# Low halves of four weight matrices kept in DRAM between two token streams, and the second prelude cut in two

## The chip, the cores and the metric

The kernel runs on one core of one Trainium2 chip. The metric is the device time of one execution in microseconds (us). A core has a matrix engine PE with a weight-load path (PEld), a vector engine DVE, a scalar engine ACT, a general engine POOL, and SP, which here issues every DMA, in program order, on one hardware queue (q1 in the profile). A DMA that waits for something on SP holds back those behind it.

## The reference

Two requests ("streams", 512 tokens by 1024 channels each, stream 0 and stream 1) go through the same two layers with the same weights. Layer 0 is a bidirectional RWKV-7 time mixing:

```python
xx = 0.5 * (x_prev + x_next) - xn
lerp = lambda j: xn + xx * mu[j]
r = heads(lerp(0) @ w_r)
k = heads(lerp(1) @ w_k)
v = heads(lerp(2) @ w_v)
z = xn @ w_z
for d in range(2):
    xw = lerp(3 + d)
    xa = lerp(5 + d)
    w_log = -softplus(-(w0[d] + tanh(xw @ w1[d]) @ w2[d])) - 0.5
    a = sigmoid(a0[d] + (xa @ a1[d]) @ a2[d])
    ys.append(_wkv7_scan(r, decay, k_d, v, -kk, kk * a, reverse=(d == 1)))
out = (norm(ys[0] + ys[1]) + bonus) * silu(z)
return out @ w_o
```

Layer 1 is a gated neighbourhood attention (w_in, four products a column block, then w_o). Each layer has an RMS norm before and after it.

## The kernel before

Activations stand with channels on the 128 partitions and 512 tokens along the row. A weight matrix of 1024x1024 is eight "columns" of 128 output channels; a column is loaded as two halves of 128x512 f32 (256 KB, tile `raw`).

A product is done in three passes of reduced precision: each operand x is split into hi = x rounded (tile `whi` for a weight, a cast on ACT) and lo = x - hi (tile `wlo`, a subtraction on DVE), and PE adds hi*hi, hi*lo and lo*hi. So a column takes 8 x 3 = 24 matmuls of 128x512, and each half column costs one cast and one subtraction. `wlo` and `whi` have four buffers each (NW = 4), `raw` three. The same weights are split once for stream 0 and again for stream 1.

The program has three parts.

**The prelude** (generator `prelude`, method `columns`). For stream s it loads x, makes the norm (sum of squares, `rstds`), the shift xx, the low-rank product (L549 to L551, 96 matmuls: tanh(xw @ w1) and xa @ a1 for both directions) with its output chain (L560 to L572: tiles `lm` and `lr`, one buffer each; the `hid` rows of stream 1 are stored from `lr`), and the shifted inputs (L581, tile `ls` of four buffers, also used for the splits of the low-rank input of stream 1), which are stored and read again later. Beside it run the eight z and the eight k columns of stream 0 (L423 to L425). A scheduler of the compiler orders this part.

**The scan phase** (`scan_phase`). Its order is recorded by hand for PE, DVE and ACT: `weave` asks a list of threads in turn, with a model clock, which can go on. Threads are the steps of the scan (8 blocks of 8 steps; L1068, L1090, L1162, L1189, L1209, L1213), `preps` (the inputs of a block: L872, L873, then DVE and ACT work up to the tile `ab`), `inverse` (a triangular inverse in many small DVE operations, L994, L996), `finish`, and `flow`, which keeps PE busy in between with the remaining products (L802 to L804): r and v of stream 0, then k, r, v and z of stream 1, then w_o and six column blocks of layer 1's w_in. In `flow` the thread `loads` fetches `raw`, `splits` casts (L721) and subtracts (L723), and `products` multiplies. If the clock foresees a gap, a dummy matmul (L1622) is put in, so that PE does not go idle. SP's DMAs are not in the hand-made order; they follow the scheduler.

**The rest** (`rest`) is the second layer and the end.

A block's preparation needs the column sums of all k columns (`rn`) and the r columns of the block; the first scan step needs the first block's preparation, its inverse and its v columns.

Of the kernel before, what the change touches and what calls it, by code (L numbers as in the profile page):

```python
# [19 lines left out]
P = 128  # L20
# [209 lines left out]
class Trunk:  # L230
# [172 lines left out]
    def split(self, raws, j):  # L403
        hi, lo = (self.t(tag, (P, self.WP), self.NW, F32R) for tag in ("whi", "wlo"))
        self.halves(raws[j], lo, hi, self.nc.vector if j % 2 else self.nc.vector)
# [85 lines left out]
    def prelude(self, s):  # L491
# [5 lines left out]
        for k in range(KT):  # L497
            if s == 0 and k == self.WFIRST:
                self.first = [self.weight(self.a["w_z"][0])]
# [36 lines left out]
        self.shift[s] = xn, xx  # L536

        pm = self.p("pf", (P, 2, T))
# [39 lines left out]
        for kind, j in (("v", 2),) if s == 0 else (("k", 1), ("r", 0), ("v", 2)):  # L578
            for k in range(KT):
                t = self.t("ls", (P, T), 4, F32, self.lp)  # L580
                vt.scalar_tensor_tensor(t, xx[k], self.vec("mu", 8 * j + k), xn[k], op0=ALU.mult, op1=ALU.add)  # L581
                self.save("l" + kind, s, k, t)
                yield
# [106 lines left out]
    def columns(self, s, kind, x, ps=range(NP)):  # L690
        for p in ps:
            w = self.first.pop() if self.first else self.weight(self.a["w_" + kind][p])
            ps = yield from self.gemm(w, x, self.gt)
            for _ in self.column(s, kind, p, ps):
                pass
            yield

    def flow(self):
# [3 lines left out]
        cols = [(g, j, src, done) for g, (_, _, c) in enumerate(self.groups) for j, (src, done) in enumerate(c)]  # L702
# [14 lines left out]
        def splits():  # L717
            for h in range(2 * len(cols)):
                yield "A", lambda: h < did["load"] and h < did["k"] // 4 + self.NW, lambda c: c.at(name(raw[h]))
                hi, lo = (self.t(tag, (P, self.WP), self.NW, F32R) for tag in ("whi", "wlo"))  # L720
                nc.scalar.copy(hi, raw[h])  # L721
                yield "D"
                nc.vector.tensor_tensor(lo, raw.pop(h), hi.bitcast(F32), op=ALU.subtract)  # L723
# [844 lines left out]
    def stream(self):  # L1568
# [3 lines left out]
            (self.a["w_" + kind][p], lambda ps, p=p: self.column(s, kind, p, ps)) for p in ps]  # L1572
# [3 lines left out]
        def x1n(k):  # L1576
# [11 lines left out]
            (now, self.xr, cols(0, "r")), (now, disk("lv", 0), cols(0, "v")), (now, disk("lk", 1), cols(1, "k")),  # L1588
# [123 lines left out]
    def run(self):  # L1712
# [85 lines left out]
def both(*gs):  # L1798
    for g in gs:
        yield from g  # L1800
# [110 lines left out]
```

## Time and profile before

| what | us |
|---|---|
| median of three runs (lowest, highest) | 1689.23 (1682.6, 1691.78) |
| the profiled execution, its own time | 1683.88 |
| its span, first to last instruction | 1682.1 |
| first matmul of the prelude | 8.8 |
| first and last start of a dummy matmul (L1622) | 171.4, 987.1 |
| first and last start of a product of the scan phase (L802) | 173.9, 1179.6 |
| DVE subtractions of weights, scan phase (L723, x160) | 108.7 |
| DVE subtractions of weights, elsewhere (L373, x148) | 101.4 |

A row of a group view reads: line, engine, operation, output<-input, shapes, count | busy us, mean ns of one | idle time of the engine just before, and what ended most of it. A row of the stage table has the stage in us, its length, and for each engine the busy time and the number of instructions, then the granted PE clock (1.00 is full), the busy share of the 16 DMA engines and the GB/s moved. A row of a timeline has the start, the length, the instruction and, in brackets, the idle time ahead of it with what ended it. A row of waits has total us, times and the longest. PE's records overlap, since a matmul starts before the one ahead of it has left the array, so the distance of two starts is what one costs.

### The profile page before, as it was taken

Reading aid. Unit: us, or ns where it says so; the run is one execution under the profiler, and the core shown is the slowest. Engines: PE = TensorE matmul, PEld = TensorE weight load, DVE = VectorE, ACT = ScalarE, POOL = GpSimd, SP = SyncE. Lnnn points to the kernel's source line nnn. Section 1 sums busy time; section 2 is a strip of 40 time slices with the busy share of each in tenths; the row PEclk is TensorE's granted clock in tenths of the full one; section 3 lists DMA queues with packets and bytes.
Section 4 is the critical chain, followed back from the end, with each engine's and each line's share of the span. In section 5 each row is a group of like instructions: output and inputs, shape, how many; then the busy total and the mean of one; then the engine's idle time right before and its main releaser. Section 6 shows DMA issues by size and latency. Waiting matters only on the chain.

```text
span 1682.1 us, 46291 instructions
## 1 busy us (share of the span) xinstructions
PE 1570.9 (93%) x18818; PEld 1201.2 (71%) x18818; DVE 1227.8 (73%) x2725; ACT 984.0 (58%) x1977; POOL 24.1 (1%) x94
## 2 busy tenths in 40 slices
PE   7989898899989998989998999999999899999998
PEld 6767666676766776767765767777777687777776
DVE  8985668688777697887888887865576856555564
ACT  5443655676655667755674665454577655555562
POOL 0000000000000000000000000000000000000000
PEclk9989999899999999999997999999999999999999
DMA  5435678678586786876776665554774347555553
GB/s 209 163 125 187 203 243 261 202 228 257 170 262 211 225 255 205 259 243 205 241 232 214 202 199 199 184 178 131 267 231 155 111 127 249 182 157 175 164 181 107
DMA packets 240821, 336.26 MB, mean 200 GB/s; under 512 B 53696, under 2 KB 119360, under 8 KB 240608
## 3 DMA queue, kind: packets, MB, share of 16 engines
q1 hardware_dynamic: 240608, 333.31, 61.6%
q8 instruction: 148, 2.42, 0.6%
q14 instruction: 65, 0.53, 0.1%
HBM read 227.71 MB, written 105.51 MB: 198 GB/s over the span
## 4 chain that ended last, share of the span: by engine, by line
PE 67%; DVE 11%; DMA 9%; ACT 8%; issue 4%; SPq 1%; DVEq 0%; POOL 0%; ACTq 0%; POOLq 0%
PE pm L802 7%; PE pg L423 6%; PE pg L424 6%; PE pg L425 6%; PE pm L804 5%; PE pm L803 5%; PE pf L1090 2%; PE sc L1433 2%; PE us L1209 2%; DMA cab<-dab 2%; PE po L1466 2%; PE pt L1451 2%; PE zy L1162 2%; PE us L1189 2%; PE zy L1213 1%
## 5 line engine op out<-in xcount | busy, mean ns | idle before, releaser
L802 PE MATMUL pm<-act,whi 128*128 128x512 f32 x640 | 287.6, 449 | 16.1 <-ACT act L771 7.2
L804 PE MATMUL pm<-act,wlo 128*128 128x512 f32 x640 | 256.7, 401 | 12.2 <-DVE wlo L723 12.2
L803 PE MATMUL pm<-act,whi 128*128 128x512 f32 x640 | 258.0, 403 | 5.1 <-DVE act L749 4.2
L423 PE MATMUL pg<-act,whi 128*128 128x512 f32 x448 | 182.4, 408 | 5.9 <-ACT act L372 5.5
L424 PE MATMUL pg<-act,whi 128*128 128x512 f32 x448 | 178.1, 398 | 0.1
L425 PE MATMUL pg<-act,wlo 128*128 128x512 f32 x448 | 177.5, 396 | 0.0
L802 PEld LDWEIGHTS pm<-act,whi 128*128 128x128 f32 x640 | 122.6, 192 | 63.8 <-issue 16.1
L372 ACT CAST whi<-raw 128x512 fp32r<-128x512 f32 x148 | 91.4, 619 | 129.3 <-PE pg L424 75.3
L804 PEld LDWEIGHTS pm<-act,wlo 128*128 128x128 f32 x640 | 123.4, 193 | 44.3 <-DVE wlo L723 16.9
L373 DVE TENSOR_TENSOR wlo<-raw,whi 128x512 fp32r<-128x512 f32 x148 | 101.4, 687 | 70.2 <-ACT whi L372 63.0
L803 PEld LDWEIGHTS pm<-act,whi 128*128 128x128 f32 x640 | 123.6, 193 | 29.6 <-DVE act L749 7.2
L723 DVE TENSOR_TENSOR wlo<-raw,whi 128x512 fp32r<-128x512 f32 x160 | 108.7, 684 | 42.9 <-ACT whi L721 39.5
L721 ACT CAST whi<-raw 128x512 fp32r<-128x512 f32 x160 | 98.1, 616 | 51.7 <-PE pm L803 14.5
L423 PEld LDWEIGHTS pg<-act,whi 128*128 128x128 f32 x448 | 84.8, 190 | 24.8 <-ACT act L372 6.1
L425 PEld LDWEIGHTS pg<-act,wlo 128*128 128x128 f32 x448 | 84.8, 189 | 17.9 <-issue 0.8
L424 PEld LDWEIGHTS pg<-act,whi 128*128 128x128 f32 x448 | 84.9, 190 | 17.4 <-issue 2.0
L996 DVE TENSOR_TENSOR N<-etmp,N 128x30 f32<-128x30 f32 (+14 forms) x240 | 78.5, 327 | 4.2
L994 DVE TENSOR_TENSOR etmp<-N 128x30 f32<-128x30 f32 (+14 forms) x240 | 78.3, 326 | 4.2
L1444 DVE CUSTOM_DVE_ANT_0 sb<-sc,bias 128x256 f32<-128x256 f32 x128 | 49.2, 419 | 31.1 <-PE pt L1451 23.5
L1090 PE MATMUL pf<-cab 64*64 64x128 f32 (+1 forms) x2048 | 67.9, 268 | 2.2 <-issue 2.1
L1447 ACT ACTIVATE sb<-sb,mx 128x256 f32<-128x256 f32 x128 | 63.9, 504 | 9.1 <-DVE mx L1446 9.0
L1113 DVE TENSOR_TENSOR AK<-zy,cc 128x256 f32<-128x256 f32 x63 | 26.6, 421 | 53.5 <-PE zy L1068 51.6
(389 smaller groups left out, 3389.7 us busy)
## 6 DMA issues: line engine op xcount, KB each, us to landing
dab<-ab SPq DMA_DIRECT2D x32, 1024.0 KB, 5.5
cab<-dab SPq DMA_DIRECT2D x64, 512.0 KB, 4.4
raw<-in_w_in_dram SPq DMA_DIRECT2D x128, 256.0 KB, 3.3
bias<-in_rpb_dram SPq DMA_DIRECT2D x32, 384.0 KB, 4.8
raw<-in_w_z_dram SPq DMA_DIRECT2D x32, 256.0 KB, 4.5
dz<-tmp SPq DMA_DIRECT2D x32, 256.0 KB, 3.0
raw<-in_w_k_dram SPq DMA_DIRECT2D x32, 256.0 KB, 4.0
dk<-tmp SPq DMA_DIRECT2D x32, 256.0 KB, 2.2
```

What stands on the lines that cost most here:

```text
L372: self.nc.scalar.copy(hi, src)
L373: (eng or self.nc.vector).tensor_tensor(lo, src, hi.bitcast(F32), op=ALU.subtract)
L423: nc.tensor.matmul(ps, hi, x[k][0], start=(k == 0), stop=False)
L424: nc.tensor.matmul(ps, hi, x[k][1], start=False, stop=False)
L425: nc.tensor.matmul(ps, lo, x[k][0], start=False, stop=(k == KT - 1))
L721: nc.scalar.copy(hi, raw[h])
L723: nc.vector.tensor_tensor(lo, raw.pop(h), hi.bitcast(F32), op=ALU.subtract)
L802: nc.tensor.matmul(ps, hi[:, at], xh, start=(k == 0), stop=False)
L803: nc.tensor.matmul(ps, hi[:, at], xl, start=False, stop=False)
L804: nc.tensor.matmul(ps, lo[:, at], xh, start=False, stop=(k == KT - 1))
L996: vt.tensor_tensor(N[:, q + 1:, :q], tv, N[:, q + 1:, :q], op=ALU.add)
L1090: end = nc.tensor.matmul(st.f[half(a), h, 0, d, g] if st.last else st.f[half(a), h, :, d, g], ab[half(h), d, g, 2 * e[d] + 1 - a], rt if s ...
```

## The change

Two things are changed.

**Low halves through DRAM.** Where stream 0 splits a half column of w_z, w_k, w_r or w_v, the low half is also stored to a DRAM tile (`lower_half`, 64 stores of 256 KB). Where stream 1 needs the same half column, `splits` loads it into `wlo` from there instead of subtracting; the cast on ACT stays, and `raw` is still loaded for it.

**The prelude.** Stream 0's prelude runs to its end first, at 0.6 of a step for each step of the z columns. Then the k columns run beside the first part of stream 1's prelude (norm, shift, the k, r and v shifts) and the v shifts of stream 0. Then the first four r columns of stream 0 run in the prelude too, written beside the low-rank product of stream 1, and the scan phase's first group has the other four.

```diff
+    PACE, EARLY = (0.95, 0.8), 4
...
+        self.wlow = {}
...
-    def weight(self, src):
+    def weight(self, src, key=None):
...
             for j in range(len(raws)):
                 out += self.split(raws, j)
+                if key:
+                    self.lower_half(key, j, self.low)
         return out
+
+    def lower_half(self, key, j, lo):
+
+        self.wlow[key, j] = d = self.dram("wl%s%d%d" % (*key, j), (P, self.WP))
+        self.nc.sync.dma_start(d, lo.bitcast(F32))
...
         self.shift[s] = xn, xx
-
+        if s == 1:
+            yield from self.shifts(1, (("k", 1), ("r", 0), ("v", 2)))
+        else:
+            yield from self.low_rank(0)
+
+    def low_rank(self, s):
...
         def splits():
             for h in range(2 * len(cols)):
-                yield "A", lambda: h < did["load"] and h < did["k"] // 4 + self.NW, lambda c: c.at(name(raw[h]))
+                key, j = keys[h // 2], h % 2
+                room = lambda: h < did["k"] // 4 + self.NW
+                yield "A" if (key, j) not in self.wlow else "S", lambda: room() and h < did["load"], (
+                    (lambda c: c.at(name(raw[h]))) if (key, j) not in self.wlow else None)
                 hi, lo = (self.t(tag, (P, self.WP), self.NW, F32R) for tag in ("whi", "wlo"))
-                nc.scalar.copy(hi, raw[h])
-                yield "D"
-                nc.vector.tensor_tensor(lo, raw.pop(h), hi.bitcast(F32), op=ALU.subtract)
+                if (key, j) in self.wlow:
+                    self.load(lo.bitcast(F32), self.wlow[key, j])
+                    yield "A", None, lambda c: c.at(name(raw[h]))
+                    nc.scalar.copy(hi, raw.pop(h))
+                else:
+                    nc.scalar.copy(hi, raw[h])
+                    yield "D"
+                    nc.vector.tensor_tensor(lo, raw.pop(h), hi.bitcast(F32), op=ALU.subtract)
+                    if key:
+                        self.lower_half(key, j, lo)
...
-            (now, self.xr, cols(0, "r")), (now, disk("lv", 0), cols(0, "v")), (now, disk("lk", 1), cols(1, "k")),
+            (now, self.xr, cols(0, "r", range(self.EARLY, NP))), (now, disk("lv", 0), cols(0, "v")), (now, disk("lk", 1), cols(1, "k")),
...
-        a = both(a, self.prelude(1))
-        run(self.columns(0, "z", self.xz), (a, 1))
-        run(self.columns(0, "k", self.shifted(0, 1)), (a, 1))
+        run(self.columns(0, "z", self.xz), (a, 0.6))
+        run(a)
+        x = self.shifted(0, 1)
+        a = both(self.prelude(1), self.shifts(0, (("v", 2),)))
+        run(self.columns(0, "k", x), (a, self.PACE[0]))
         run(a)
         self.xr = self.shifted(0, 0)
+        a = self.low_rank(1)
+        run(self.columns(0, "r", self.xr, range(self.EARLY)), (a, self.PACE[1]))
+        run(a)
         first.close()
```

The order of the built programs shows where this puts the work. In these rows a tile's number tells its buffers apart.

PE, at the end of the prelude, in the kernel before: L646 is the last operation of a k column, L1622 the dummy, L802 to L804 the first r column (pm_1734), L872 and L873 the first matmuls of the first preparation.

```order
L646 MATMUL pm_1626<-tmp_1624,cc 2x512
L1622 MATMUL zy_1710<-cc 128x256 x6
L802 MATMUL pm_1734<-act_1641,whi_1725 128x512
L803 MATMUL pm_1734<-act_1640,whi_1725 128x512
L804 MATMUL pm_1734<-act_1641,wlo_1726 128x512
...
L804 MATMUL pm_1774<-act_1683,wlo_1803 128x512
L1622 MATMUL zy_1710<-cc 128x256 x2
L872 MATMUL pm_1835<-h_126_633,w2h_1793 128x512
L873 MATMUL pm_1835<-h_126_633,w2l_1792 128x512
```

The same place in the changed kernel: L433 to L435 end the fourth r column, L568 to L570 are the low-rank product of stream 1 (pf_1614, pm_1615, us_1616), L835 to L837 the fifth r column, L905 and L906 the first preparation.

```order
L435 MATMUL zy_1893<-act_1588,wlo_1888 128x512
L1655 MATMUL zy_1954<-cc 128x256 x6
L568 MATMUL pf_1614<-ls_1617,lw_359 128x512
L568 MATMUL pm_1615<-ls_1617,lw_345 128x512
L568 MATMUL us_1616<-ls_1617,lw_395 128x512
L835 MATMUL pm_1995<-act_1546,whi_1984 128x512
...
L570 MATMUL pf_1614<-ls_1822,lw_421 128x512
L569 MATMUL us_1616<-ls_1823,lw_399 128x512
L570 MATMUL us_1616<-ls_1822,lw_400 128x512
L905 MATMUL pm_2014<-h_172_797,w2h_1972 128x512
L906 MATMUL pm_2014<-h_172_797,w2l_1971 128x512
```

The low-rank product of stream 1, which lay among the k columns, now lies in one piece behind the fourth r column, with the first 12 matmuls of the fifth among it, and the first preparation follows at once.

DVE, at the same time, in the kernel before: L563, L565 and L570 are the output chain of the low-rank product, L581 the shifts, L599 and L373 the r operands, L854 and L858 open the first preparation.

```order
L570 TENSOR_TENSOR lr_1277<-pm_1050,lm_1276 128x512
L581 SCALAR_TENSOR_TENSOR ls_1434<-xx_988,cv,xn_759 128x512
...
L563 TENSOR_TENSOR lr_1297<-lm_1296 128x512
L373 TENSOR_TENSOR act_1652<-xr_1650,act_1653 128x512
L599 SCALAR_TENSOR_TENSOR xr_1662<-xx_402,cv,xn_119 128x512
...
L570 TENSOR_TENSOR lr_1297<-us_1051,lm_1296 128x512
...
L854 SCALAR_TENSOR_TENSOR rb_1788<-k_1786,cv,rb_1788 128x512
L858 TENSOR_TENSOR w2l_1792<-tmp_1794,w2h_1793 128x512
```

In the changed kernel (L603 the shifts, L375 the splits of the low-rank input, L582, L584 and L589 the output chain, L887 and L891 the preparation):

```order
L603 SCALAR_TENSOR_TENSOR ls_1512<-xx_525,cv,xn_141 128x512
L375 TENSOR_TENSOR ls_1618<-xn_892,ls_1617 128x512
...
L375 TENSOR_TENSOR ls_1823<-xn_906,ls_1822 128x512
L582 TENSOR_TENSOR lr_1848<-lm_1847 128x512
L584 SCALAR_TENSOR_TENSOR lm_1847<-lr_1848,lm_1847 128x512
L589 TENSOR_TENSOR lr_1848<-pm_1615,lm_1847 128x512
L582 TENSOR_TENSOR lr_1872<-lm_1871 128x512
L584 SCALAR_TENSOR_TENSOR lm_1871<-lr_1872,lm_1871 128x512
L589 TENSOR_TENSOR lr_1872<-us_1616,lm_1871 128x512
L1675 COPY mrx_1937<-cc 128x128 x2
L887 SCALAR_TENSOR_TENSOR rb_1967<-k_1965,cv,rb_1967 128x512
L891 TENSOR_TENSOR w2l_1971<-tmp_1973,w2h_1972 128x512
```

The output chain, which lay spread among shifts and splits, now stands in one piece between the low-rank splits and the preparation.

SP, where stream 1's k columns are fetched, in the changed kernel: a load of a stored low half (`dwlk`) stands beside the load of `raw`, in the queue that also brings the scan's inputs (cab, V, X).

```order
L330 DMA cab_518_1943<-dab_526_1964 128x1024
L330 DMA V_4274<-dvt_680_2552 128x256
L330 DMA wlo_4289<-dwlk_258_1068 128x512
L327 DMA dk_993_4314<-tmp_4312 128x512
L330 DMA raw_4317<-in_w_k_dram 128x512
L330 DMA xr_5404<-dlr_319_1268 128x512
L330 DMA wlo_4370<-dwlk_274_1131 128x512
L330 DMA wlo_4430<-dwlk_277_1137 128x512
```

Over the whole program PE has the same matmuls but for 81 dummies instead of 97; up to the first scan step (the first L1209, L1242 in the change) it has 324 products of the scan phase and 44 dummies before, 264 and 41 now, and behind the last full step (all but the last of a block) 69 and 93 products. DVE has 64 subtractions of weights fewer, and SP 64 stores and 64 loads more.

More of the change, by code (lines that the diff above doesn't have):

```diff
@@ L404, in split @@
         hi, lo = (self.t(tag, (P, self.WP), self.NW, F32R) for tag in ("whi", "wlo"))
-        self.halves(raws[j], lo, hi, self.nc.vector if j % 2 else self.nc.vector)
+        self.halves(raws[j], lo, hi)
+        self.low = lo
         return [(hi[:, k * P:(k + 1) * P], lo[:, k * P:(k + 1) * P]) for k in range(self.WP // P)]
-    def weight(self, src):
+    def weight(self, src, key=None):
         out = []
@@ L577, in prelude, with shifts @@
             yield
-        for kind, j in (("v", 2),) if s == 0 else (("k", 1), ("r", 0), ("v", 2)):
+    def shifts(self, s, kinds):
+        xn, xx = self.shift[s]
+        for kind, j in kinds:
             for k in range(KT):
                 t = self.t("ls", (P, T), 4, F32, self.lp)
-                vt.scalar_tensor_tensor(t, xx[k], self.vec("mu", 8 * j + k), xn[k], op0=ALU.mult, op1=ALU.add)
+                self.nc.vector.scalar_tensor_tensor(t, xx[k], self.vec("mu", 8 * j + k), xn[k], op0=ALU.mult, op1=ALU.add)
                 self.save("l" + kind, s, k, t)
@@ L701, in flow @@
         nc, did, ck = self.nc, self.did, self.clock
-        cols = [(g, j, src, done) for g, (_, _, c) in enumerate(self.groups) for j, (src, done) in enumerate(c)]
+        cols = [(g, j, src, done) for g, (_, _, c) in enumerate(self.groups) for j, (src, done, *_) in enumerate(c)]
+        keys = [key[0] if key else None for _, _, c in self.groups for _, _, *key in c]
         name = lambda *xs: [x.tensor.name for x in xs]
@@ L1571, in stream @@
         cols = lambda s, kind, ps=range(NP): [
-            (self.a["w_" + kind][p], lambda ps, p=p: self.column(s, kind, p, ps)) for p in ps]
+            (self.a["w_" + kind][p], lambda ps, p=p: self.column(s, kind, p, ps), (kind, p)) for p in ps]
         disk = lambda kind, s: lambda k: self.load(self.t("xr", bufs=self.NXR), sp[kind, s, k])
```

7 lines of the change are left out of this document (5 added, 2 removed).

## Prediction

> **What bounds the kernel now.** I read the engines' busy shares first, then the chain that ended last, then a table of stages, then who waits for whom in the long stage.
>
> ```profile
> PE 1570.9 (93%) x18818; PEld 1201.2 (71%) x18818; DVE 1227.8 (73%) x2725; ACT 984.0 (58%) x1977; POOL 24.1 (1%) x94
> PE 67%; DVE 11%; DMA 9%; ACT 8%; issue 4%; SPq 1%; DVEq 0%; POOL 0%; ACTq 0%; POOLq 0%
> ```
>
> PE is the bound on average, yet a third of the chain lies elsewhere. The stages say where:
>
> ```profile
> core 0: us, PE busy (x) PEld busy (x) DVE busy (x) ACT busy (x) POOL busy (x), PEclk, DMA share, GB/s
> 82.00:102.00 20.00, 14.12 (x43) 9.65 (x42) 19.08 (x35) 12.08 (x20) 0.13 (x2) 0.66 0.24 87
> 102.00:144.00 42.00, 42.00 (x172) 30.62 (x171) 23.49 (x39) 13.79 (x24) 0.00 (x0) 1.00 0.31 110
> 144.00:175.00 31.00, 28.82 (x117) 20.21 (x117) 26.55 (x41) 14.45 (x26) 0.13 (x2) 1.00 0.78 273
> 175.00:192.00 17.00, 13.64 (x51) 9.96 (x49) 7.69 (x15) 9.05 (x18) 3.61 (x3) 0.90 0.77 245
> 192.00:321.00 129.00, 113.09 (x1184) 86.33 (x1184) 93.96 (x167) 84.97 (x163) 2.80 (x10) 0.96 0.71 225
> 321.00:600.00 279.00, 258.51 (x4799) 190.65 (x4800) 217.52 (x433) 179.57 (x359) 4.81 (x13) 0.97 0.72 223
> 600.00:880.00 280.00, 258.82 (x4433) 197.90 (x4426) 228.78 (x446) 185.91 (x364) 5.06 (x15) 0.96 0.75 237
> 880.00:1161.00 281.00, 266.32 (x4890) 200.70 (x4890) 211.45 (x414) 149.15 (x282) 6.02 (x9) 0.96 0.59 192
> ```
>
> Up to 175 is the prelude, 175 to 321 the preparation of the first scan block, 321 to 1161 the scan; behind it lie left-over products and the second layer, which the change does not touch. In the scan PE is busy for 258.51 + 258.82 + 266.32 = 783.7 of 840 us: 56 us idle. Part of the busy time is no work either, since the planner fills forecast gaps with dummy matmuls (L1622):
>
> ```profile
> 192.00:321.00 129.00, 17.66 (x72) 13.52 (x72) 0.96 0.71 225
> 321.00:1161.00 840.00, 29.55 (x106) 22.66 (x106) 0.97 0.69 217
> ```
>
> ```profile
> PE pm L804 <- DVE wlo L723: 8.5, 4, 3.5
> PE zy L1068 <- DMA cab<-dab: 3.6, 2, 2.4
> ```
>
> So of the scan's idle time, the splits' subtraction on DVE, which the change removes for stream 1, ends 8.5 us directly.
>
> **The change part by part.** PE's useful work is the same in both kernels: the four r columns move from the scan to the prelude, and the low-rank product of stream 1 (96 matmuls) moves the other way, behind them. The time can change only by PE's idle, half-clock and dummy time, so I add these stage by stage.
>
> (1) Prelude to the end of r column 3. These rows give the pace:
>
> ```profile
> 82.08 0.39 PE L423 MATMUL zy<-act,whi 128*128 128x512 f32 x1
> 85.77 0.50 PE L424 MATMUL zy<-act,whi 128*128 128x512 f32 x1 [2.34 <-DVE act L373]
> 99.24 0.63 PE L423 MATMUL zy<-act,whi 128*128 128x512 f32 x1
> 99.67 0.63 PE L424 MATMUL zy<-act,whi 128*128 128x512 f32 x1
> 102.47 0.39 PE L423 MATMUL zy<-act,whi 128*128 128x512 f32 x1
> 102.69 0.39 PE L424 MATMUL zy<-act,whi 128*128 128x512 f32 x1
> ...
> 171.69 2.54 PE L1622 MATMUL zy<-cc 128*128 128x256 f32 x11
> 179.80 0.50 PE L802 MATMUL pm<-act,whi 128*128 128x512 f32 x1 [2.81 <-ACT whi L721]
> 191.25 0.50 PE L872 MATMUL pm<-h,w2h 128*128 128x512 f32 x1 [0.33 <-ACT w2h L856]
> ```
>
> ```profile
> L646 PE MATMUL pm<-tmp,cc 128*2 128x512 f32 x16 | 8.2, 592 | 2.2 <-ACT tmp L642 2.2
> L463 PE MATMUL pm<-tmp,ones 128*128 128x128 f32 x16 | 3.4, 362 | 2.5 <-DVE tmp L459 2.5
> L451 PE MATMUL pm<-ones,acc 128*128 128x1 f32 x8 | 1.8, 351 | 0.0
> ```
>
> Matmuls start 0.2275 us apart (24 of them, a column, take 5.5), but 0.43 after PE has stalled (the granted clock is 0.66 in that stage). The k columns begin at 82.1. From there the kernel before does 8 k columns and the low-rank product, 288 matmuls, and the changed one 8 k and 4 r columns, also 288: 65.5 us, plus 8.2 (L646), plus 3.5 for the norm of stream 1 (half of L463, and L451). That would end at 159.3; before, it ends at 171.7, 12 us later, because the k operands come late from a DVE that is busy 19.08 of 20 us. In the changed order the v shifts are behind the k operands and two k columns share each operand as it comes, so I leave 2 us of this: 161, a gain of 10.7 (bounds: 0, if the operands are as late as before, and 12.4).
>
> (2) The join. The low-rank splits now stand on DVE behind all shifts of stream 1 and the v shifts of stream 0; 15 shifts follow the last r split, each waiting for a buffer of a ring of four that its store must leave.
>
> ```profile
> L581 DVE SCALAR_TENSOR_TENSOR ls<-xx,cv,xn x24: 739/744/752, 143.8 to 173.8; 128x512 f32<-128x512 f32 x24
> ```
>
> ```profile
> dk<-tmp SPq DMA_DIRECT2D x32, 256.0 KB, 2.2
> ```
>
> In 144 to 175 24 shifts took 30 us, 1.25 each. The last r split needs the buffer that r column 1 leaves, at 161 - 11 = 150. Then 15 x 1.25 = 19 us, and one reload of a value just stored (2.2) ahead of the first cast: the low-rank product starts at 172, PE idle for 11 us. Bounds: 161 (stores hidden), and 183 if the 34 transfers of 0.26 MB left on SP run at the 273 GB/s of 144 to 175. With the 12 products among it the block takes 108 x 0.2275 = 24.6, plus 2 at half clock (9 matmuls at 0.43): 198.6.
>
> (3) Behind it stands, on DVE and ACT alike, the low-rank output, and only then the first preparation; no other work is between. It is a serial chain with one buffer:
>
> ```profile
> 154.45 0.68 DVE L570 TENSOR_TENSOR lr<-pm,lm 128x512 f32<-128x512 f32 x1
> ...
> 166.17 0.69 DVE L563 TENSOR_TENSOR lr<-lm 128x512 f32<-128x512 f32 x1
> ```
>
> ```profile
> 156.59 0.61 ACT L572 ACTIVATE lr<-lr 64x512 f32<-64x512 f32 x1
> ...
> 161.95 0.63 ACT L572 ACTIVATE lr<-lr 64x512 f32<-64x512 f32 x1 [3.52 <-DMA dhid<-lr]
> ```
>
> ```profile
> L454 ACT ACT_TABLE_LOAD x2 | 2.6, 1283 | 0.0
> ```
>
> Before, the two halves of it lay 12 us apart and other work hid that. Now the cover is gone: copy 0.9, three DVE operations 2.1, table load and tanh 1.9, then three stores of the hidden rows that the next step waits for, with activations of 0.6 and three more DVE operations (2.1) between them, and the cast of w2: 9.7 plus the stores. A store costs 4.7 above (157.2 to 161.95, DMA at 0.78) and 2.2 in the page; I take 2.5, as the queue is then nearly empty: 17 us (16.3 to 23). The first preparation matmul stands at 215.6 instead of 191.25, 24.3 later, with 60 more matmuls done (13.7): parts (1) to (3) lose 10.7 us together.
>
> The Trainium skill, "DMA: Bandwidth & Descriptors", section "Anatomy of one DMA", fits a transfer as about 2.0 us plus bytes over 436 GB/s, most of it the write's receipt (for the software queue, not this one); that estimate is 2.3 us for these 128 KB, the loss would be 10.1, and the trace's 4.7 shows how far a filled queue is from it.
>
> (4) Preparation to the first scan step.
>
> ```profile
> L1209 PE MATMUL us<-X,Tm x896: 221/222/369, 323.6 to 1156.6; 128*64 128x64 f32 x180
> ```
>
> It took 132 us (191.25 to 323.6) with 276 products and 38 dummies; the changed order has 252 and 35 there: 6.7 us less on PE (a dummy is 0.42: the row at 171.69 holds six of them, two records each with one missing). If the chain of preparation sets the pace, as 16 idle and 17.7 dummy us of 129 suggest, this room is lost; 24 stores of low halves also join a queue at 0.71. I take +4 (0 to 12).
>
> (5) Scan. Between the first and the last step there are 60 products fewer and 40 dummies instead of 53: the products were done elsewhere, the dummies are a gain of 5.5. The subtraction is this row:
>
> ```profile
> L723 DVE TENSOR_TENSOR wlo<-raw,whi 128x512 fp32r<-128x512 f32 x160 | 108.7, 684 | 42.9 <-ACT whi L721 39.5
> ```
>
> Of its 160 calls 72 are gone, 64 by loads and 8 with the moved columns: 45% of the 8.5 us, 3.8. Against it 64 loads of 256 KB on the one SP queue, ahead of cab and X: at least 0, at most the 56 us of idle growing by 0.2 us per load (13); I take 4. Together -5.5 (-28, half of all idle and no late load, to +13).
>
> Sum: +10.7 + 4 - 5.5 = +9.2 on the profiled execution's 1683.88, 1693. That execution lies 5.35 under the median of the three runs (1689.23), so 1698.
>
> **The rivals.** *DVE was the hidden pace-maker* (faster). DVE is busy 657.8 of 840 us in the scan; taking 49 us off it (72 x 0.684) could end half of the 56 idle us, many of which end at ACT or at operands behind DVE. Then (5) is -28 and (4) 0: -17, about 1672. For it: 8.5 us end directly at the subtraction. Against it: only one in seven idle us does. It decides if the join costs less than 28.
>
> *SP becomes the wait* (slower still).
>
> ```profile
> SPq L328 <- DVE wlo L723: 86.2, 62, 7.3
> ```
>
> SP already stands 86 us behind this subtraction, to reload raw; now 24 stores in the first 130 us of the scan phase stand behind it too, and 64 loads behind PE's release of a buffer, with cab, V and X queued after them. If (4) is +12 and (5) +13, it is +36: about 1725. The Trainium skill, the page on DMA above, same section, says a semaphore wait happens on the issuing sequencer, never in the DMA engines; the trace agrees, the 86.2 us are SP's own.
>
> *The join is free* (no change). If the shifts' stores keep up and the low-rank product starts at 161, with the chain behind it at its 16.3, (1) to (3) gain 1 and the sum is -2.5: 1687. For it: DVE alone needs only 15 x 0.75 us for the shifts. Against it: the 1.25 us that 24 of them took, and the order of the stores on SP, where low halves now lie between. That the loads replace nothing is excluded: DVE has 64 subtractions fewer in the order.
>
> **How the numbers follow.** Forecast 0.50, DVE 0.22, SP 0.17, free join 0.11. A measurement can tell about 0.5%, 8.4 us, from no change: faster is below 1680.8, slower above 1697.7. The forecast, with its own range 1688 to 1710, is slower in 0.31, same in 0.17, faster in 0.02; SP is slower; DVE is faster; the free join is same in 0.09, faster in 0.02. So faster 0.26, same 0.26, slower 0.48. The range reaches to both outer rivals, 1670 to 1725, a little past the one and up to the other.
>
> **What would show it.** Right: PE idle for some 10 us ahead of the low-rank product of stream 1 and 15 or more behind it, with the half clock after each; the first preparation matmul at 210 to 220; the first scan step at 340 or later, and from there to the last step some 20 us less than the 833 before. Wrong: no gap at the join; a stage of scan shorter by 40 us; or matmuls L837 (the low half) waiting for DMA in many places, which would mean SP.

## The result, and the profile after

The change makes the kernel slower by 2.8%: a median of 1735.41 us (1733.98 to 1739.3, four runs) against 1688.74 (1682.6 to 1691.78, four runs), ratio 1.0281, 95% interval 1.0254 to 1.0308. The profiled execution took 1736.81 us, against 1683.88 before: 52.9 more, and the stages below are read against that. The page first (engine, busy us, share, instructions):

```profile
PE 1565.4 (90%) x18786; PEld 1201.7 (69%) x18786; DVE 1200.5 (69%) x2661; ACT 981.2 (57%) x1975; POOL 24.1 (1%) x94
```

PE is busy for 5.5 us less than before and DVE for 27.3 less, in a longer run. Nothing was added to the engines. What grew is their idle time, and the bytes moved: the DMA queue carried 366.87 MB against 333.31. The stages of the changed kernel, in the columns of the prediction's table:

```profile
82.00:166.00 84.00, 78.44 (x316) 56.15 (x315) 71.80 (x118) 43.60 (x78) 0.26 (x4) 0.96 0.75 256
166.00:179.00 13.00, 3.83 (x16) 2.73 (x15) 7.50 (x11) 1.82 (x3) 0.00 (x0) 0.86 0.94 337
179.00:208.00 29.00, 26.12 (x108) 21.05 (x107) 7.62 (x11) 6.52 (x10) 0.13 (x2) 0.94 0.09 35
208.00:221.00 13.00, 0.00 (x0) 0.00 (x0) 2.35 (x5) 3.96 (x10) 0.00 (x0) 0.56 0.16 35
221.00:354.00 133.00, 112.84 (x1177) 87.52 (x1178) 91.75 (x163) 83.08 (x161) 6.28 (x12) 0.93 0.86 269
354.00:1197.00 843.00, 756.36 (x13928) 570.65 (x13927) 623.47 (x1221) 508.09 (x996) 16.00 (x38) 0.96 0.73 233
1197.00:1734.90 537.90, 515.14 (x2947) 405.16 (x2943) 330.37 (x993) 295.51 (x658) 0.00 (x0) 0.98 0.53 171
```

And of the kernel before, with the same three cuts (first preparation matmul, first and last scan step):

```profile
191.00:324.00 133.00, 116.61 (x1266) 88.79 (x1268) 96.69 (x172) 87.26 (x168) 2.80 (x10) 0.96 0.69 220
324.00:1157.00 833.00, 776.65 (x13957) 584.09 (x13953) 654.11 (x1285) 512.40 (x1001) 15.89 (x37) 0.97 0.69 218
1157.00:1682.10 525.10, 506.68 (x2923) 399.56 (x2919) 326.15 (x989) 292.93 (x653) 0.00 (x0) 0.99 0.54 173
```

The first preparation matmul comes 30 us later (221.4 against 191.25), and this is not made up anywhere: the preparation takes the same 133 us with 24 products fewer, the scan 10 us more with 60 fewer (PE idle 86.6 against 56.4 us), and what follows the last scan step 12.8 us more, with 24 products more. The dummies fell by 7 us in the scan (29.55 before) and not at all ahead of it (windows with their line alone):

```profile
221.00:354.00 133.00, 18.91 (x70) 14.32 (x70) 0.93 0.86 269
354.00:1197.00 843.00, 22.43 (x80) 15.13 (x80) 0.96 0.73 233
```

At the join both gaps of the prediction are there. Who waited for whom on PE, 150 to 230 us:

```profile
PE pm L905 <- ACT w2h L889: 16.2, 1, 16.2
PE pf L568 <- ACT ls L374: 8.5, 1, 8.5
```

L568 is the low-rank product of stream 1, L905 the first preparation matmul. The DMA issues on SP over the same time (start, duration):

```profile
178.42 0.50 SPq L327 DMA_DIRECT2D dlv<-ls  x1
208.35 11.77 SPq L327 DMA_DIRECT2D dhid<-lr  x4
220.22 1.18 SPq L330 DMA_DIRECT2D rb<-drn  x2
221.45 0.58 SPq L330 DMA_DIRECT2D k<-dk  x1
```

Ahead of 179 the DMA engines are 94% busy. PE waits for a cast on ACT there, and ACT in turn for the DMAs; the last of these rows, later, is a step of the serial chain that waits 2.33 us for its store:

```profile
176.38 0.62 ACT L780 CAST act<-xr 128x512 fp32r<-128x512 f32 x1 [9.15 <-DMA xr<-dlv]
177.97 0.62 ACT L374 CAST ls<-xn 128x512 fp32r<-128x512 f32 x1 [0.97 <-DMA dlv<-ls]
219.02 0.63 ACT L591 ACTIVATE lr<-lr 64x512 f32<-64x512 f32 x1 [2.33 <-DMA dhid<-lr]
```

Then SP issues nothing for 30 us (share 0.09), because the next store in its order waits for the low-rank output. The loads of the first preparation (`rb`, `k`) stand behind the four stores and start at 220. From 221 on the share is 0.86, against 0.69 before.

### The profile page after: what moved, and what is told of

It reads as the page before. It is cut to its first block, busy times and chain, and to the rows that moved or that the text cites. A ratio compares the mean times of both kernels' runs of the same rounds, so it can differ in the third digit from the quotient of the medians.

```text
span 1734.9 us, 46463 instructions
## 1 busy us (share of the span) xinstructions
PE 1565.4 (90%) x18786; PEld 1201.7 (69%) x18786; DVE 1200.5 (69%) x2661; ACT 981.2 (57%) x1975; POOL 24.1 (1%) x94
## 3 DMA queue, kind: packets, MB, share of 16 engines
q1 hardware_dynamic: 259040, 366.87, 65.4%
## 5 line engine op out<-in xcount | busy, mean ns | idle before, releaser
L835 PE MATMUL pm<-act,whi 128*128 128x512 f32 x608 | 272.8, 449 | 9.2 <-ACT act L780 2.8
L837 PE MATMUL pm<-act,wlo 128*128 128x512 f32 x608 | 244.0, 401 | 7.1 <-DVE wlo L754 6.6
L836 PE MATMUL pm<-act,whi 128*128 128x512 f32 x608 | 244.0, 401 | 3.4 <-DVE act L782 1.8
L433 PE MATMUL pg<-act,whi 128*128 128x512 f32 x448 | 183.8, 412 | 3.1 <-ACT os L1523 1.9
L435 PE MATMUL pg<-act,wlo 128*128 128x512 f32 x448 | 178.8, 399 | 0.0
L374 ACT CAST whi<-raw 128x512 fp32r<-128x512 f32 x156 | 96.3, 618 | 144.3 <-PE pg L434 76.3
L835 PEld LDWEIGHTS pm<-act,whi 128*128 128x128 f32 x608 | 117.4, 193 | 55.1 <-issue 16.1
L375 DVE TENSOR_TENSOR wlo<-raw,whi 128x512 fp32r<-128x512 f32 x156 | 107.2, 689 | 69.4 <-ACT whi L374 61.6
L837 PEld LDWEIGHTS pm<-act,wlo 128*128 128x128 f32 x608 | 117.1, 193 | 38.1 <-DVE wlo L754 9.6
L836 PEld LDWEIGHTS pm<-act,whi 128*128 128x128 f32 x608 | 118.1, 194 | 23.9 <-DVE act L782 3.4
L433 PEld LDWEIGHTS pg<-act,whi 128*128 128x128 f32 x448 | 85.2, 190 | 21.7 <-issue 3.2
L435 PEld LDWEIGHTS pg<-act,wlo 128*128 128x128 f32 x448 | 85.3, 191 | 18.2 <-issue 0.8
L433 PE MATMUL zy<-act,whi 128*128 128x512 f32 x160 | 64.6, 409 | 9.6 <-ACT whi L374 9.1
L754 DVE TENSOR_TENSOR wlo<-raw,whi 128x512 fp32r<-128x512 f32 x88 | 60.1, 685 | 18.8 <-ACT whi L752 18.7
L1234 ACT COPY X<-us 64x256 f32<-64x256 f32 x128 | 46.9, 366 | 46.2 <-PE zy L1101 44.8
```

The lines of the kernel that those rows point to most:

```text
L374: self.nc.scalar.copy(hi, src)
L375: (eng or self.nc.vector).tensor_tensor(lo, src, hi.bitcast(F32), op=ALU.subtract)
L433: nc.tensor.matmul(ps, hi, x[k][0], start=(k == 0), stop=False)
L435: nc.tensor.matmul(ps, lo, x[k][0], start=False, stop=(k == KT - 1))
L835: nc.tensor.matmul(ps, hi[:, at], xh, start=(k == 0), stop=False)
L836: nc.tensor.matmul(ps, hi[:, at], xl, start=False, stop=False)
```

## The experiments

Eighteen kernels ran. Code is shown in part, with "..." where lines are left out, and as a difference from the changed kernel unless the text says otherwise. A ratio is to the kernel before, whose median was between 1682.6 and 1688.7 in each set of runs. L-numbers are those of each kernel's own listing.

### Each part alone

e1_prelude keeps the new prelude and drops the low halves in DRAM.

```diff
-                if key:
-                    self.lower_half(key, j, self.low)
...
-                    if key:
-                        self.lower_half(key, j, lo)
```

> The changed kernel without low halves in DRAM: no stores in the first stream, both streams subtract on DVE as before; the new prelude stays. In the changed kernel the first preparation matmul came 30.2 us later than before with 13.7 us more product work done, so the join costs about 16; the scan then took 9 us longer with 60 products (13.7 us) fewer, so about 23 more. Theory SP (waits of the halves' stores and loads on the one queue make the scan late) and theory bytes (40 MB more traffic makes all transfers late) both put the scan's 23 on the halves: 1705 here, the scan at 820 or less. Theory prelude (everything comes from the new order ahead of the scan): 1730 or more. Theory plan (the planner's order happens to be worse with another set of columns): anything, and the scan's idle time not at transfers.

Measured: 1723.86, ratio 1.0222 (1.0189 to 1.0255). With the prelude alone four fifths of the loss are there. Its scan is not at 820 but at 841.2, so the scan's loss is not the halves' only.

e2_halves keeps the halves and restores the order of the prelude.

```diff
-    PACE, EARLY = (0.95, 0.8), 4
+    EARLY = 0
...
+        a = both(a, self.prelude(1))
+        run(self.columns(0, "z", self.xz), (a, 1))
+        run(self.columns(0, "k", self.shifted(0, 1)), (a, 1))
```

> The prelude as before, the four r columns back in the scan, but the low halves of the r, k, v, z weights stored by the first stream and loaded by the second. Theories SP and bytes: before plus the scan's loss, 1689 + 23 = 1712, up to 1720. Theory prelude: 1689 or a little below (64 subtractions fewer on DVE). Theory plan: between, with the loss in blocks that differ from those of the changed kernel.

Measured: 1730.5, ratio 1.0274 (1.0227 to 1.0321), above what any of the theories said. The two parts cost 2.2% and 2.7% alone and 2.8% together: they do not add up.

e3_stores is the changed kernel with stores, without loads (stream 1 subtracts).

```diff
-                if (key, j) in self.wlow:
+                if False:
...
-                    if key:
+                    if key and (key, j) not in self.wlow:
```

> The changed kernel with the stores of the low halves, but the second stream subtracts on DVE and loads none. Theory SP: the stores wait for DVE only in the prelude and the first 130 us of the scan phase, the loads wait for PE in the rest, so most of the scan's loss goes with the loads: about 1712. Theory bytes: half of the traffic remains, all of it early: the preparation ahead of the first scan step stays at about 133 us and the scan recovers, 1715. Theory prelude: 1730 or more.

Measured: 1734.48, ratio 1.0295 (1.0262 to 1.0327). With the stores alone the whole loss is there, so 64 loads in the place of 64 subtractions change nothing that shows. That can be two costs of nothing or two that cancel, and as this scan has another order, it holds to about 1% only. When the halves are moved in the changed kernel the trace shows (first and last start of an issue):

```profile
L425 SPq DMA_DIRECT2D dwlv<-wlo x16: 319/391/1429, 256.2 to 340.9; - x16
L330 SPq DMA_DIRECT2D wlo<-dwlk x16: 319/383/1688, 338.2 to 452.5; - x16
L330 SPq DMA_DIRECT2D wlo<-dwlz x16: 319/392/1604, 719.1 to 920.8; - x16
```

The v halves are the last ones stored, so the stores lie ahead of the first scan step (354.2), and the halves that move during the scan are loads. In e3_stores, where no half moves during the scan, the scan takes 847 us, in its own order.

e4_poolq moves the halves' transfers to another queue; a further edit, not shown, keeps the planner's order as it was.

```diff
-        self.nc.sync.dma_start(d, lo.bitcast(F32))
+        self.nc.gpsimd.dma_start(d, lo.bitcast(F32))
...
-                    self.load(lo.bitcast(F32), self.wlow[key, j])
+                    nc.gpsimd.dma_start(lo.bitcast(F32), self.wlow[key, j])
```

> The changed kernel with the stores and loads of the low halves on POOL's DMA queue instead of SP's; the order on PE, DVE and ACT in the scan stays as it is, and the bytes stay. Theory SP: nothing stands behind their waits on SP any more, the scan loses its 23 us: about 1710. Theory bytes: 1735, as the traffic is the same. Theory prelude: 1735. POOL's own memsets of the preparation now stand behind the stores; if that costs, the time is above 1735.

Measured: 1738.4 (1725.72 to 1740.53), ratio 1.0305 (1.0265 to 1.0345). No gain in the median. The profiled execution is the fastest of the four by 11 us, and its scan took 832.9, 10 less than in the changed kernel; the slower three have no trace. So the median does not support the rival in which SP's queue sets the time, and this one trace leaves it possible.

### How much an order is worth

`weave` records another order after any small edit. Four kernels move one constant of it and nothing else (p1 and p2 in the kernel before, p3 and p4 in the changed one). AHEADE is the lead that the planner gives each engine; p2 moves that of ACT and DVE from 200 to 250 ns.

```diff
-    NZ1, STOCK, EPS, NEAR = 6, 1, 60.0, 400.0
+    NZ1, STOCK, EPS, NEAR = 6, 1, 50.0, 400.0
```

> The kernel before with one planner constant moved, EPS 60 to 50: same instructions, same traffic, only another order in the scan phase. Theory plan (the order of before is a lucky one among its neighbours, and any change of the set of columns throws another): 15 to 40 above before, 1700 to 1725, in the scan. Theories SP, bytes and prelude: within 8 of before, 1677 to 1693, as nothing that they name is changed.

```diff
-    AHEADE = dict(S=3000.0, A=200.0, D=200.0)
+    AHEADE = dict(S=3000.0, A=250.0, D=250.0)
```

> The kernel before with the planner's lead on ACT and DVE moved from 200 to 250 ns: same instructions and traffic in another order, one whose end the planner itself puts 14 us earlier. Theory plan: 1700 to 1725 all the same. Theories SP, bytes and prelude: within 8 of before; if the planner's own times were to be believed, 1671.

```diff
-    NZ1, STOCK, EPS, NEAR = 6, 1, 60.0, 400.0
+    NZ1, STOCK, EPS, NEAR = 6, 1, 70.0, 400.0
```

> The changed kernel with EPS 60 to 70, nothing else. Theory plan: the changed kernel is an average draw, so this one lies on either side of 1735, 1715 to 1750. Theories SP, bytes, prelude: 1727 to 1743.

```diff
-    WARM = 300.0
+    WARM = 350.0
```

> The changed kernel with the planner's bound for dummy matmuls at 350 instead of 300 ns. Theory plan: on either side of 1735, 1715 to 1750. Theories SP, bytes, prelude: 1727 to 1743.

Measured: p1_before_eps50 1695.38, ratio 1.0050 (1.0026 to 1.0075); p2_before_lead 1673.77, ratio 0.9929 (0.9891 to 0.9967); p3_after_eps70 1716.0, ratio 1.0165 (1.0129 to 1.0201); p4_after_warm 1726.33, ratio 1.0221 (1.018 to 1.0261). An order alone moves a kernel by 0.7% down to 0.5% up (before) and by 0.6 to 1.1% down (changed); for the kernel before that is more than "within 8" and less than "15 to 40". The order of the changed kernel is the slowest of those that ran, so a part of its 2.8%, perhaps 1%, is bad luck. Not all of it is: the fastest order of the changed kernel (1.0165) is still 1.1% over the slowest of the kernel before (1.0050). A loss below 1% is read only from pairs that share an order. p2_before_lead beats both kernels.

Two kernels repeat the comparison at that better setting, the changed kernel and e1_prelude, each with the AHEADE line above.

> The changed kernel with the planner's lead on ACT and DVE at 250 instead of 200 ns, the setting with which the kernel before fell to 1674. If the change costs a fixed amount whatever the order, 1674 + 40 = 1714; if the order of the changed kernel is only an unlucky one, below 1700.

> The new prelude without the low halves in DRAM, with the planner's lead at 250. If the prelude's 38 are the prelude's own, 1674 + 38 = 1712; if they were an unlucky order, 1674 plus the join as measured ahead of the scan (8.5 of the prelude and 3 of the preparation), 1686 to 1695.

Measured: l1_after_lead 1718.38, ratio 1.0204 (1.0174 to 1.0233); l2_prelude_lead 1711.75, ratio 1.0160 (1.013 to 1.0189). Against p2_before_lead's 0.9929 that is 2.8% and 2.3%: the same losses as at the old setting, so they belong to the change.

### Bytes, and what a product is worth

e7_short keeps the order and the waits and takes the bytes away: each transfer moves 8 of its 512 columns, so the products of stream 1 read old low halves. Edits that are not shown keep the planner's times and the ring of `wlo` as they were.

```diff
-        self.nc.sync.dma_start(d, lo.bitcast(F32))
+        self.nc.sync.dma_start(d[:, 0:8], lo.bitcast(F32)[:, 0:8])
...
-                    self.load(lo.bitcast(F32), self.wlow[key, j])
+                    self.load(lo.bitcast(F32)[:, 0:8], self.wlow[key, j][:, 0:8])
```

> The changed kernel in its own order on PE, DVE and ACT, with every store and load of a low half cut to 8 of its 512 columns (so the products of the second stream read old low halves); the 152 transfers, their queue and their waits stay, 39 of their 40 MB go. Theory bytes: the scan loses its extra 20 to 30 us of idle time and the prelude ends 8 earlier, 1700 to 1710. Theory waits (SP standing behind DVE and PE): 1727 to 1735, only the prelude's 8 may go. Theory chain (the scan's length is set by its own chain of steps, and products taken out only leave holes): 1725 to 1735.

(There are 128 transfers of 33.6 MB, not 152 of 40.) Measured: 1720.66, ratio 1.0211 (1.0173 to 1.0248): 0.7% less than the changed kernel, and between the expectations. Its preparation and scan, the first preparation matmul now at 217.3:

```profile
217.00:348.00 131.00, 114.53 (x1180) 89.06 (x1182) 91.66 (x163) 83.47 (x161) 6.27 (x12) 0.91 0.75 225
348.00:1181.00 833.00, 751.26 (x13920) 567.60 (x13922) 623.04 (x1220) 507.79 (x995) 16.00 (x38) 0.96 0.69 216
```

Read from one traced execution of each, the bytes cost 4 us in the prelude, 2 in the preparation and 10 in the scan, where the only halves moved are loads. Half of them is idle time of PE (86.6 against 81.7 us), half is longer matmuls (756.36 against 751.26 us busy, with the same work). Without the bytes the scan is as long as before (833), with 60 products fewer: the products taken out still gained nothing. The longest wait of PE in the changed kernel's scan is one for late data, DVE and then PE (start, duration, idle before and its cause):

```profile
786.05 0.69 DVE L1312 TENSOR_TENSOR bv<-pm,bv 128x512 f32<-128x512 f32 x1 [6.31 <-DMA bv<-dv]
```

```profile
786.79 1.11 PE L1318 MATMUL pm<-cc,y 128*128 128x128 f32 x4 [5.79 <-DVE bv L1312]
```

This is not the bytes' doing, since the same wait is there in e7_short:

```profile
771.61 0.69 DVE L1313 TENSOR_TENSOR bv<-pm,bv 128x512 f32<-128x512 f32 x1 [5.46 <-DMA bv<-dv]
```

Over the scan DVE waits for this load for 17.9 us in the kernel before, 18.5 in the changed one and 15.7 in e7_short. Which waits make up the 10 us stays open.

e8_fewer prices a product in the scan: the order of before, with 80 matmuls taken out of it. The cut is against the kernel before; `ghost` makes the planner count each of them as if it were there.

```diff
+                    if k == 3:
+                        ck.ghost = 1
+                    else:
+                        nc.tensor.matmul(ps, lo[:, at], xh, start=False, stop=(k == KT - 1))
...
+        for _ in range(self.ghost):
+            t = max([self.t["P"]] + list(self.tiles.values()))
+            self.tiles[0, 0], self.t["P"], end = t + 227.0, t + 6.5, max(end, t + 437.0)
+        self.ghost = 0
```

> The kernel before in its own order, with one product matmul of 24 left out of each of the 80 columns of the scan phase (the low half of the fourth block of rows is missing in the result), while the planner still counts it: 80 matmuls, 18.2 us of PE, some 61 of them between the first and the last scan step. It prices the term of the prediction that put 60 products fewer in the scan at 13.7 us less. Theory PE-bound: 1687 - 18 = 1669. Theory chain: the holes are left as idle time, 1680 to 1687.

Measured: 1691.6, ratio 1.0041 (1.0016 to 1.0066): slower, outside both expectations. Preparation and scan:

```profile
191.00:327.00 136.00, 117.78 (x1240) 89.38 (x1241) 95.99 (x171) 86.69 (x167) 2.80 (x10) 0.92 0.69 215
327.00:1161.00 834.00, 762.51 (x13881) 571.72 (x13882) 654.22 (x1285) 512.63 (x1001) 15.89 (x37) 0.97 0.69 218
```

In the scan PE is busy for 14.1 us less than in the row of before (762.51 against 776.65) and the stage is 1 us longer; in the preparation the granted clock fell from 0.96 to 0.92. The stretch behind the scan, 529.0 against 525.5, is longer too. The holes stay (PE idle 71.5 us in the scan against 56.4), and PE is not what sets the length of the scan in this order.

### The two halves of the prelude

e9_early adds the four r columns to the old prelude; e10_late is the new order without them. From the preparation on, e9_early has the recorded order of e1_prelude, and e10_late that of the kernel before. Neither has low halves in DRAM. e9_early is shown against the kernel before.

```diff
         run(self.columns(0, "k", self.shifted(0, 1)), (a, 1))
         run(a)
         self.xr = self.shifted(0, 0)
+        run(self.columns(0, "r", self.xr, range(self.EARLY)))
```

> The prelude in the order of before, with the four r columns added at its end; no low halves in DRAM. From the first preparation on its order is that of e1_prelude. Theory free products (in the scan a product fills a hole and its removal gives nothing back, ahead of the scan each costs its 0.2275 us): the prelude is 96 x 0.2275 = 22 longer, the rest as in e1_prelude, so 1715 to 1725, as e1_prelude. Theory order (the shifts and the late low-rank product are what costs): 1685 to 1695.

> As e9_early with the planner's lead at 250, so the scan's order is that of l2_prelude_lead (1712). Theory free products: 1702 to 1712. Theory order: 1674 to 1685.

```diff
-    PACE, EARLY = (0.95, 0.8), 4
+    PACE, EARLY = (0.95, 0.8), 0
```

> The new prelude with no r column in it (EARLY 0) and no low halves; from the first preparation on its order is that of the kernel before. Theory free products: the prelude falls back to some 191 to 205 (the low-rank product waits for the shifts with nothing to cover it), the rest is as before: 1685 to 1700. Theory order: the 38 us stay, 1715 or more.

Measured: e9_early 1703.14, ratio 1.0101 (1.0071 to 1.013); e9_early_lead 1690.37, ratio 1.0020 (0.9998 to 1.0043), 0.9% over p2_before_lead; e10_late 1716.04, ratio 1.0181 (1.0149 to 1.0213). Neither theory alone: the early columns cost 1.0% and the order 1.2% on top (1.0222 less 1.0101; 1.4% at the other setting). Preparation, scan and the rest of e9_early, then of e1_prelude:

```profile
200.00:326.00 126.00, 115.01 (x1260) 89.42 (x1260) 93.27 (x167) 86.84 (x170) 2.80 (x10) 0.93 0.76 234
326.00:1167.00 841.00, 772.71 (x13913) 580.35 (x13911) 656.99 (x1287) 508.75 (x993) 15.89 (x37) 0.96 0.68 215
1167.00:1702.90 535.90, 509.72 (x2933) 401.99 (x2931) 323.64 (x985) 293.79 (x651) 0.00 (x0) 0.97 0.51 167
```

```profile
213.00:346.00 133.00, 117.99 (x1248) 90.87 (x1250) 94.90 (x170) 87.89 (x172) 6.40 (x13) 0.89 0.76 232
346.00:1187.00 841.00, 778.53 (x13925) 584.70 (x13926) 657.48 (x1287) 509.46 (x993) 15.91 (x37) 0.96 0.68 215
1187.00:1723.60 536.60, 510.88 (x2931) 402.49 (x2927) 323.73 (x984) 292.95 (x651) 0.00 (x0) 0.97 0.52 167
```

From the first scan step on the two are alike; the order's 20 us lie ahead of it, at 326 against 346. In e9_early itself the columns cost nothing up to there (324 before, with 48 products more done); the cost is that a scan with 12 products fewer lasts 9 us longer and the stretch behind it, with 36 fewer, 11 longer. In e10_late, with no column as cover, PE's gaps at the join are 16.7 and 15.6 us, and the order alone costs the 1.8%.

e12_lowrank and e13_repaired move the low-rank product of stream 1 back beside the k columns, and the shifts beside the r columns, without and with the halves.

```diff
-        if s == 1:
-            yield from self.shifts(1, (("k", 1), ("r", 0), ("v", 2)))
-        else:
-            yield from self.low_rank(0)
+        yield from self.low_rank(s)
...
-        a = both(self.prelude(1), self.shifts(0, (("v", 2),)))
+        a = self.prelude(1)
...
-        a = self.low_rank(1)
+        a = both(self.shifts(0, (("v", 2),)), self.shifts(1, (("k", 1), ("r", 0), ("v", 2))))
```

> e1_prelude (1724) with the low-rank product of stream 1 back beside the k columns, ahead of the shifts, which now run beside the r columns; scan order unchanged. Theory late product: PE's two gaps (8.5 ahead of the product, 13 behind it) and the idle DMA queue of 30 us go, the first scan step comes at some 326 as in e9_early instead of 346, total 1700 to 1708. Theory other edits: 1718 or more.

> The changed kernel, low halves included, with the same repair, its scan order unchanged. Theory late product: 1735 less 20, 1710 to 1718, so what is left above 1687 is the halves and the scan. Theory other edits: 1728 or more. If the stores of the low halves then meet the shifts' stores on SP with no gap to drain in, part of the gain is lost: 1720.

Measured: e12_lowrank 1712.69, ratio 1.0147 (1.0116 to 1.0177), against 1.0222; e13_repaired 1721.41, ratio 1.0200 (1.017 to 1.0231), against 1.0281. The first scan steps come at 332.8 and 339.0 instead of 345.9 and 354.2. So the late product is 0.75 and 0.8% of the loss, about two thirds of the order's part. The rest of the join in e12_lowrank, 82 to 215 us on PE:

```profile
PE pm L899 <- DVE w2l L884: 6.6, 1, 6.6
PE pm L898 <- ACT w2h L882: 5.7, 1, 5.7
```

### The halves on the old prelude

l3_halves_lead is e2_halves with the AHEADE line.

> The low halves in DRAM with the prelude of before, lead 250. At lead 200 they cost 45 alone, with a scan that the planner itself put 23 longer. If that was the order's bad luck, here 1674 + 10 = 1684 to 1690; if the halves cost it themselves, 1710 to 1720.

Measured: 1729.03, ratio 1.0262 (1.0227 to 1.0298), 3.4% over p2_before_lead: the halves alone are dear at both settings, so it is not the bad luck of one order. Scan and what follows it, up to the second layer:

```profile
329.00:1140.00 811.00, 741.05 (x13848) 556.87 (x13847) 607.47 (x1197) 499.60 (x980) 16.01 (x38) 0.95 0.75 239
1140.00:1217.00 77.00, 76.27 (x415) 60.64 (x410) 39.96 (x77) 32.80 (x56) 0.00 (x0) 1.00 0.58 197
```

Here the recorded order leaves 297 products for after the last scan step (69 before), 77 us of nothing but PE work; in e2_halves the scan itself is 881 us. Both fill the scan badly, and nothing that was run says why this costs 2.7% and more here, but only 0.6% on the new prelude (1.0281 less 1.0222).

## Why the prediction was right and wrong

The sign was right, the time was 37 us too low, and beyond the range. On the profiled execution the miss is 43.7 us (1736.81 against 1693.1), and by the prediction's own steps it lies here:

| step | predicted | measured |
|---|---|---|
| (1) end of r column 3 | 161 | 166 (last pass starts at 165.8) |
| (2) low-rank product starts; PE idle | 172; 11 | 178.6; 9.2 |
| (3) first preparation matmul | 215.6 | 221.4 |
| (4) first scan step (215.6 + 132.4 + 4) | 352 | 354.2 |
| (5) first to last scan step (833 - 13.65 - 5.5) | 814 | 842.4 |
| behind the last step, against before | 0 | +12.8 |

**Steps (1) to (4) hold** in their mechanism: the first scan step is 2 us from the forecast, though that close by luck, since errors of a few us cancel. The join has its two gaps for the reasons given: DMA at 0.94 with PE waiting ahead of the low-rank product, then the serial chain (16.2 us of wait; 17 forecast, with 2.5 for each store, which took 2.3 to 2.4). e12_lowrank and e13_repaired show that the late product costs 13 to 15 us ahead of the scan. The r columns ended 5 us late, so the first preparation matmul stands just outside the 210 to 220 that were named, while (4), put at 4 longer, was level. What the sum did not see is that the first preparation's own loads stand on SP behind the stores of that chain; it is inside the measured 133 us, and no run priced it alone.

**Step (5) is the one that failed**, by 28 us. It took the profile's view that PE bounds the scan (93% busy) and gave each product that left the scan its 0.2275 us, and each dummy its 0.42: 19 us of gain ("some 20 us less than the 833"). e8_fewer shows the price of a product there: 80 of them out, 18.2 us of PE, and the kernel does not get faster, it gets 0.4% slower. e7_short agrees: without the bytes the changed order has 25 us less of busy PE in its scan and takes the same 833. The idle 56 us and the dummies in the scan were the sign of it: where a planner has to fill holes, a filler that is taken away leaves the hole. The prediction drew this conclusion for the preparation in (4), and not for the scan. Which chain sets the length of the scan in PE's place no run shows.

The other 10 us of the miss are traffic, in this order of the scan. Term (5) had 4 us for late loads and took 3.8 back for DVE (its three terms add up to -5.3, put down as -5.5). e7_short shows 10 us in the scan for the bytes of the loads, and nothing shows that the subtraction gave anything back. The stores, which end ahead of the first scan step, can act only before it: e3_stores reaches that step at 350.6, e1_prelude at 345.9. What stays open is the scan of e1_prelude and e9_early: with 12 products fewer and no half moved, but in another order, it takes 841 us, 8 more than before.

**Behind the last step** the sum had nothing. The changed order leaves 93 products there instead of 69; 24 x 0.2275 is 5.5 of the 12.8. The rest is not traced, but l1_after_lead, with 69 left, has 528.5 us there, 3 more than before, so it hangs on the order.

**The rivals.** DVE as hidden pace-maker: wrong; DVE is busy for 31 us less in the scan (623.47 against 654.11) and nothing follows. e7_short, with neither these subtractions nor the bytes, is at 1.0211 where e1_prelude, with the subtractions and in another order, is at 1.0222. SP as the wait: its time (1725) was nearest, its mechanism is not shown. Its sign is missing: in the scan L837 waits 5.9 us for DVE and never for a DMA. With the halves' transfers on POOL's queue nothing is gained in the median, while with the waits kept and the bytes gone 0.7% is. Whether bytes of the same size cost less on another queue stays open, as the one traced execution of e4_poolq had the short scan. The free join: wrong, both gaps are there.

Put together by ratios along a chain of kernels, before to e9_early to e1_prelude to the changed one: early columns 1.0%, the prelude's order 1.2% (0.8% of it the late product), low halves 0.6%. Each step carries about 0.3% of uncertainty and, in the first and last, another order of the scan, which is worth up to 1%.

## What to carry to other kernels

A matmul is worth its length only in a stage where removing it shortens the stage: idle time and dummy matmuls in a "busy" stage say that another chain sets its pace, and then taking work out of it buys nothing. Where a planner records an order, first move one of its constants and see how far the time moves; compare edits in pairs that share an order. A transfer that replaces an operation of an engine with slack bought nothing here and was paid in the bytes.

## What was not expected of the hardware

Taking PE work out made a kernel slower, by 0.4% (e8_fewer, 1.0016 to 1.0066). The granted clock went with it: in its preparation it was 0.92 against 0.96, and in the join of the changed kernel 0.56 while PE stood still for 13 us. What a hole costs afterwards can be read in the starts of the matmuls behind the gap ahead of the low-rank product:

```profile
178.64 0.80 PE L568 MATMUL pf<-ls,lw 128*128 128x512 f32 x1 [8.50 <-ACT ls L374]
179.23 0.63 PE L568 MATMUL pm<-ls,lw 128*128 128x512 f32 x1
179.66 0.63 PE L568 MATMUL us<-ls,lw 128*128 128x512 f32 x1
```

The starts are 0.43 us apart up to 182.22 and 0.23 from there on, so this hole was paid with its idle time and with some 1.8 us of slow matmuls. Over whole runs (span, mean granted clock), before, changed, and p2_before_lead, the fastest:

```profile
core 0: 1682.1 us, clock 0.971
```

```profile
core 0: 1734.9 us, clock 0.961
```

```profile
core 0: 1669.9 us, clock 0.974
```

The slower kernel has the lower clock here, and within one kernel too (e1_prelude: 1716.32 us at 0.960, 1726.79 at 0.953). Which of the two is the cause no run separates. The Trainium skill, "TensorE: Matmul & The Clock Gate", "Part 1: The HAM clock gate", says that the half rate is the default and that a window of some 3.4 us of idleness brings it back; the 0.56 over an idle stretch of 13 us agrees.
